# One group's store on GpSimd's queue: three transfers become seven, with other partition counts per DMA engine

## The chip, the cores and the metric

The kernel runs on one core of a Trainium2 chip. Its time is the device time of one execution in microseconds (us); below it is told as the median of several runs. The profile is one further execution, taken by the hardware profiler. Besides the compute engines (TensorE, VectorE, ScalarE, GpSimd and SyncE, in the profile PE, DVE, ACT, POOL and SP) the core has 16 DMA engines. They move all data between the chip's memory and the core's on-chip memory, and every transfer is spread over some or all of them.

## The reference

```python
x: (8, 16, 256, 512) float32      # 128 matrices of 256 x 512
weight: (8, 16, 512, 384) float32 # 128 matrices of 512 x 384
out = np.matmul(x, weight)        # 128 matrices of 256 x 384
```

In all 167.8 MB are read and 50.3 MB are written.

## The kernel before, in words

The 128 matrices are handled in 32 groups of four (`NG = 32`, `G = 4`), numbered n = 0 to 31. For each group SyncE loads 2 MB of x (`load_x`, line 121) and 3 MB of weights (`load_w`, line 138; in two halves for the first four and last two groups). VectorE casts x to bfloat16 (line 194) and, with ScalarE, the weights (lines 207 and 223). TensorE transposes x through PSUM (line 247) and multiplies (line 265, and line 283 for the last group). ScalarE copies the transposed x (line 234) and the products (`copy_out`, line 300) out of PSUM, and the group's 1.5 MB of results are stored (`store`, line 160). The engines run freely beside each other and are held together by semaphores alone.

The order of the transfers is written out by hand in `on_sync`: x of group n + 4, the store of group n, the weights of group n + 4, in a loop; then x and weights of groups 30 and 31; then the stores of groups 27, 28, 29, 30 and 31 (`LAG = 4`). All of these go through SyncE's DMA queue, and each spreads its 128 partitions over the 16 DMA engines, eight partitions to each.

One store is not in that list: that of group 26, the sixth from the end (`SHARED = NG - 2 - LAG = 26`). GpSimd issues it (`store_rest`, lines 164 to 179), when ScalarE has copied the last products of group 26 out and the store of group 25 has landed. It is cut by partitions into three transfers of 5, 120 and 3 partitions. A partition holds 8 rows of 384 numbers, which is 12288 bytes; `max_dma_last_dim` cuts that into two packets of 6144 bytes. Ahead of the first and the third transfer, `reset_dge_cursor` sets back the cursor that says on which DMA engine GpSimd's next transfer begins. All three count up one semaphore, `rest_out`.

The results lie in a ring of four slots (`OS = 4`), so that group 30 writes where group 26 lay. `copy_out` of group 30 therefore waits for `rest_out` to reach 16 for each of the transfers (line 296) before its first copy. GpSimd has nothing to do after `store_rest`.

At the end, SyncE waits for the landing of the stores of groups 28 to 30 (`o_end`, line 329), counts a spare semaphore up some times (lines 330 to 333, `PAD = 12`), and waits for the landing of the last store (`o_fin`).

Of the kernel before, what the change touches and what calls it, by code (L numbers as in the profile page):

```python
# [12 lines left out]
def kernel(  # L13
# [10 lines left out]
    _, _, _, N = weight.shape  # L24
# [18 lines left out]
    R = G * M // P  # L43
    T = R // 2
    SH, SL = 2, 4
    NG = B // G
# [5 lines left out]
    LAG = 4  # L52
# [6 lines left out]

    PAD = 12  # L60

    SHARED = NG - 2 - LAG

    ctx.enter_context(tc.tile_critical(sync_engine=mybir.EngineType.Pool, no_gpsimd_drain=True))  # L64

    def sbuf(name, shape, dtype, n):
        return [
            ctx.enter_context(nc.sbuf_tensor(f"{name}{s}", shape, dtype)) for s in range(n)
        ]
# [6 lines left out]
    def sems(name, n):  # L76
        return [tc.alloc_semaphore(f"{name}{s}") for s in range(n)]
# [9 lines left out]
    out_sb = sbuf("out_sb", [P, OS * R, N], fp32, 1)[0]  # L87
# [16 lines left out]
    rest_out = sems("rest_out", 1)[0]  # L104
# [59 lines left out]
    def store_rest(e):  # L164
        n = SHARED
        e.wait_ge(o_copied, n * T + T + BIAS)
        e.wait_ge(o_out[(n - 1) % 2], 16 + 16 * ((n + 1) // 2))
        dram = o_rows[n * G * M : (n + 1) * G * M].rearrange("(p r) n -> p r n", r=R)
        a = slot(0, NG, n) * R
        p = 0  # L170
        for k, reset in ((5, True), (120, False), (3, True)):
            if reset:
                e.inc_swdge_sem([], [], mode="reset_dge_cursor")
            e.dma_start(  # L174
                out=dram[p : p + k],
                in_=out_sb[p : p + k, a : a + R],
                max_dma_last_dim=R // 2 * N * 4,
            ).then_inc(rest_out, 16)
            p += k

    def is_shared(n):
        return isinstance(n, int) and n == SHARED

    def slot(t, U, s):
        return (t * U + s) % OS
# [106 lines left out]
    def copy_out(e, t, U, s, q):  # L292
        n = t * U + s
        if q == 0:
            if isinstance(n, int) and is_shared(n - OS):
                e.wait_ge(rest_out, 16 * 3)
            elif not isinstance(n, int) or n >= OS:
                e.wait_ge(o_out[s % 2], (t * (U // 2) + s // 2) * 16 + (16 - OS // 2 * 16 + 16))
        e.wait_ge(p_made, n * T + (q + 1 + BIAS))
        e.copy(  # L300
            out=out_sb[:, bass.ds(slot(t, U, s) * R + 2 * q, 2), :],
            in_=po[(s * T + q) % PO][:, :, :N],
        ).then_inc(o_copied, 1)

    def on_gpsimd(e):
        e.memset(identity[:], 0.0).then_inc(id_done, 1)  # L306
        e.wait_ge(id_done, 1)
        make_identity(nc, identity[:], nomemset=True)
        e.drain().then_inc(id_done, 1)
        store_rest(e)  # L310
# [70 lines left out]
    def on_scalar(e):  # L381
# [8 lines left out]
        def step(t, U, s):  # L390
            short = is_short(t * U + s + 1)
            evacuate(e, t, U, s + 1, range(T - 1))
            for q in range(T):
                copy_out(e, t, U, s, q)
                if q == 0:
                    evacuate(e, t, U, s + 1, range(T - 1, T))
                if q == 0 and short:
                    e.sem_inc(w_acast, CA)
                if q > 0 and not short:
                    last = CA if q == T - 1 else q  # L400
                    cast_w(e, t, U, s + 1, range(CV + q - 1, CV + last), q == 1)
# [11 lines left out]
        for q in range(T):  # L413
            copy_out(e, 0, NG, NG - 1, q)
# [36 lines left out]
```

## Time and profile before

| what | value |
|---|---|
| median of 3 runs | 515.9 us (515.87 to 516.13) |
| the profiled execution | 515.93 us, of which the span from first to last instruction is 514.2 us |
| busy share of the span | ScalarE 80%, VectorE 77%, TensorE 61%, GpSimd 1% |
| moved by DMA | 218.18 MB, 424 GB/s over the span |
| SyncE's DMA queue | 98.8% of the time of 16 engines over the span |
| GpSimd's DMA queue | 368 packets, 1.57 MB, 0.7% |
| GpSimd's three issues | 460.5 to 463.6 us |
| issue of the last store (SyncE) | 505.50 us |

The table is read so: the page of the profile gives the busy time of each compute engine, and for DMA the time that each queue's packets took, as a share of what 16 engines could have worked in the span. Times in the text are us from the start of the span.

### The profile page before, as it was taken

How to read it: one execution, taken by the hardware profiler on the slowest of the kernel's cores; microseconds unless marked ns; L12 is line 12 of the kernel's file. 1: busy time of each engine (PE TensorE's matmuls, PEld its weight loads, DVE VectorE, ACT ScalarE, POOL GpSimd, SP SyncE). 2: the span in 40 equal slices, each digit the busy share in tenths (PEclk: the TensorE clock that was granted, in tenths of full speed). 3: DMA queues.
4: the chain of work that ended last, by engine and by line, in shares of the span. 5: the costliest groups of instructions: out<-in, count | busy, mean ns of one | idle time of the engine just before them, and what ended most of it. 6: DMA issues, size and time to landing. Idle time of an engine off the chain costs nothing.

```text
span 514.2 us, 11663 instructions
## 1 busy us (share of the span) xinstructions
PE 312.7 (61%) x4512; PEld 220.0 (43%) x4512; DVE 397.6 (77%) x462; ACT 409.6 (80%) x387; POOL 3.8 (1%) x9
## 2 busy tenths in 40 slices
PE   2276737546575656865666754577547576655872
PEld 2254425434354443543444543445434354442551
DVE  2788757797777887778977779777798777887980
ACT  1365577897987997898989799879897987998662
POOL 0000000000000000000000000000000000010000
PEclk9698878777876887686778687878777886878697
DMA  8999999999999999999999999999999999999997
GB/s 335 430 427 422 441 422 425 432 431 437 428 422 434 432 431 435 423 428 433 437 429 433 422 434 434 431 432 422 433 437 434 429 427 429 431 436 421 422 429 306
DMA packets 15686, 218.18 MB, mean 424 GB/s; under 512 B 1728, under 2 KB 1728, under 8 KB 3008
## 3 DMA queue, kind: packets, MB, share of 16 engines
q1 hardware_dynamic: 15312, 216.54, 98.8%
q0 software_dynamic: 368, 1.57, 0.7%
q8 instruction: 3, 0.05, 0.0%
q14 instruction: 3, 0.02, 0.0%
HBM read 167.77 MB, written 50.33 MB: 424 GB/s over the span
## 4 chain that ended last, share of the span: by engine, by line
DMA 55%; DVE 31%; issue 9%; PE 1%; DVEq 1%; SPq 1%; ACT 0%; POOLq 0%
DMA w_sb<-in_weight_dram 55%; DVE w_bf L207 20%; DVE w_bf L223 5%; DVE x_bf L194 5%; PE po L283 1%; SPq L138 0%; DVEq L358 0%; SPq L121 0%; DVEq L64 0%; DVEq L203 0%; ACT out_sb L300 0%; SPq L133 0%; DVEq L191 0%; DVEq L217 0%; SPq L446 0%
## 5 line engine op out<-in xcount | busy, mean ns | idle before, releaser
L207 DVE CAST w_bf<-w_sb 32x1536 bf16<-32x1536 f32 x286 | 271.9, 951 | 81.7 <-DMA w_sb<-in_weight_dram 70.5
L265 PE MATMUL po<-w_bf,x_t 128*32 128x384 bf16 x3968 | 194.6, 355 | 35.2 <-DVE w_bf L207 23.3
L247 PE MATMUL pt<-identity,x_bf 128*128 128x128 f32 x512 | 113.1, 409 | 155.2 <-DVE x_bf L194 155.2
L207 ACT CAST w_bf<-w_sb 32x1536 bf16<-32x1536 f32 x130 | 190.9, 1468 | 5.1 <-DMA w_sb<-in_weight_dram 2.0
L247 PEld LDWEIGHTS pt<-identity,x_bf 128*128 128x128 f32 x512 | 101.6, 223 | 167.5 <-issue 167.0
L265 PEld LDWEIGHTS po<-w_bf,x_t 128*32 128x32 bf16 x3968 | 115.4, 104 | 112.9 <-issue 50.0
L300 ACT COPY out_sb<-po 128x768 f32 (+1 forms) x128 | 102.4, 800 | 59.3 <-PE po L265 54.1
L234 ACT COPY x_t<-pt 128x1024 bf16<-128x1024 bf16 x128 | 123.5, 1020 | 20.6 <-PE pt L247 20.0
L194 DVE CAST x_bf<-x_sb 128x1024 bf16<-128x1024 f32 x128 | 80.0, 688 | 12.4 <-DMA x_sb<-in_x_dram 11.6
L223 DVE CAST w_bf<-w_sb 64x1536 bf16<-64x1536 f32 x48 | 45.8, 955 | 7.3 <-DMA w_sb<-in_weight_dram 6.0
L234 ACT ACT_TABLE_LOAD x1 | 1.3, 1283 | 10.8 <-PE pt L247 10.8
L174 POOL DMA_DIRECT2D out_dram<-out_sb x3 | 3.1, 1040 | 458.7 <-DMA out_dram<-out_sb 458.7
L283 PE MATMUL po<-w_bf,x_t 128*128 128x384 bf16 x32 | 5.4, 326 | 1.6 <-DVE w_bf L223 1.6
L283 PEld LDWEIGHTS po<-w_bf,x_t 128*128 128x128 bf16 x32 | 3.1, 98 | 3.9 <-issue 1.9
masks.py:199 POOL TENSOR_SCALAR_AFFINE_SELECT identity<-identity 128x128 f32<-128x128 f32 x1 | 0.3, 284 | 0.2 <-POOL identity L306 0.2
L306 POOL MEMSET identity<- 128x128 f32 x1 | 0.2, 205 | 0.5 <-POOLq L64 0.5
L435 POOL MEMSET const-bfloat16-1.0<- 128x1 bf16 x1 | 0.1, 97 | 0.0
L435 POOL MEMSET const-uint8-127<- 128x1 uint8 x1 | 0.1, 97 | 0.0
L435 POOL MEMSET const-float32-0.0<- 128x1 f32 x1 | 0.1, 93 | 0.3 <-issue 0.3
L435 POOL MEMSET const-float32-1.0<- 128x1 f32 x1 | 0.1, 93 | 0.0
## 6 DMA issues: line engine op xcount, KB each, us to landing
w_sb<-in_weight_dram SPq DMA_DIRECT2D x26, 3072.0 KB, 18.1
x_sb<-in_x_dram SPq DMA_DIRECT2D x32, 2048.0 KB, 22.2
out_dram<-out_sb SPq DMA_DIRECT2D x31, 1536.0 KB, 24.9
w_sb<-in_weight_dram SPq DMA_DIRECT2D x12, 1536.0 KB, 16.7
out_dram<-out_sb POOLq DMA_DIRECT2D x1, 1440.0 KB, 17.0
out_dram<-out_sb POOLq DMA_DIRECT2D x1, 60.0 KB, 7.3
out_dram<-out_sb POOLq DMA_DIRECT2D x1, 36.0 KB, 17.9
```

What stands on the lines that cost most here:

```text
L174: e.dma_start(out=dram[p : p + k], in_=out_sb[p : p + k, a : a + R], max_dma_last_dim=R // 2 * N * 4,).then_inc(rest_out, 16)
L194: e.tensor_copy(out=x_bf[s % BS][:, rows].rearrange("p r (s q c) -> p r s q c", s=S, c=KO), in_=x_sb[s % XS][:, rows].rearrange("p r (q s ...
L207: copy(out=w_bf[(s * G + i) % WBS][h * C : (h + 1) * C], in_=w_sb[s % WS][i * C : (i + 1) * C, h * KO : (h + 1) * KO, :],).then_inc(w_vcas ...
L223: e.tensor_copy(out=w_bf[(n * G + d * SH + a) % WBS][h * p : (h + 1) * p], in_=w_sb[n % WS][a * p : (a + 1) * p, r : r + KO, :],).then_inc ...
L234: e.copy(out=x_t[s % TS][:, 2 * q : 2 * q + 2], in_=pt[(s * T + q) % PT][:].bitcast(bf16),).then_inc(t_copied, 1)
L247: ins = e.transpose(pt[(s * T + q) % PT][:, rr, h, :], words[:, 2 * q + rr, h :: KO // 2], identity[:],)
L265: ins = e.matmul(po[(s * T + q) % PO][mine, rr, :N], x_t[s % TS][:, 2 * q + rr, ko // 2, mine, ko % 2], w_bf[(s * G + i) % WBS][:, ko, :], ...
L283: ins = e.matmul(po[(s * T + q) % PO][:, rr, :N], x_t[s % TS][:, 2 * q + rr, ko // 2, :, ko % 2], w_bf[(s * G + q) % WBS][:, ko, :], start ...
L300: e.copy(out=out_sb[:, bass.ds(slot(t, U, s) * R + 2 * q, 2), :], in_=po[(s * T + q) % PO][:, :, :N],).then_inc(o_copied, 1)
L306: e.memset(identity[:], 0.0).then_inc(id_done, 1)
L435: nc = _bacc.Bacc("TRN2", target_bir_lowering=False, num_devices=1)
```

## The change

The 128 partitions of group 26 are cut into seven transfers instead of three. Each line says whether the cursor is set back first, the first partition, the number of partitions, and which of the partition's eight rows are taken. The first five partitions are stored in two halves of four rows each. The wait in `copy_out` counts seven transfers. The few words that come with the change name the engines 1 to 16: engines 13 to 16 get six partitions, 6 to 12 ten, and the first four eight.

```diff
-    SHARED = NG - 2 - LAG
+    SHARED, PARTS = NG - 2 - LAG, 7
...
-        p = 0
-        for k, reset in ((5, True), (120, False), (3, True)):
+        H = R // 2
+        parts = [
+            (True, 0, 5, 0, H),
+            (False, 5, 75, 0, R),
+            (True, 0, 5, H, R),
+            (False, 80, 35, 0, R),
+            (False, 115, 8, 0, R),
+            (True, 123, 4, 0, R),
+            (True, 127, 1, 0, R),
+        ]
+        assert len(parts) == PARTS
+        for reset, p, k, lo, hi in parts:
             if reset:
                 e.inc_swdge_sem([], [], mode="reset_dge_cursor")
             e.dma_start(
-                out=dram[p : p + k],
-                in_=out_sb[p : p + k, a : a + R],
-                max_dma_last_dim=R // 2 * N * 4,
+                out=dram[p : p + k, lo:hi],
+                in_=out_sb[p : p + k, a + lo : a + hi],
+                max_dma_last_dim=(hi - lo) // 2 * N * 4,
             ).then_inc(rest_out, 16)
-            p += k
...
-                e.wait_ge(rest_out, 16 * 3)
+                e.wait_ge(rest_out, 16 * PARTS)
```

## The prediction

> **What bounds the kernel now.** I read the page's DMA rows first.
>
> ```profile
> DMA  8999999999999999999999999999999999999997
> ...
> q1 hardware_dynamic: 15312, 216.54, 98.8%
> q0 software_dynamic: 368, 1.57, 0.7%
> ```
>
> The DMA engines are full in every slice but the first and the last. The bytes are fixed, so time can only be lost where some engines have work left and others have none. That is the end, which the windows show (busy us of PE, PEld, DVE, ACT and POOL, clock, DMA share, GB/s):
>
> ```profile
> 500.00:505.00 5.00, 4.64 (x29) 2.56 (x27) 0.00 (x0) 2.72 (x4) 0.00 (x0) 1.00 1.01 430
> 505.00:510.00 5.00, 0.00 (x0) 0.00 (x0) 0.00 (x0) 0.47 (x1) 0.00 (x0) 0.85 0.96 393
> 510.00:514.20 4.20, 0.00 (x0) 0.00 (x0) 0.00 (x0) 0.00 (x0) 0.00 (x0) 0.50 0.24 96
> ```
>
> No compute engine works after 505.5; 7 us more are DMA. The DMA view of 509.2 to 513.2 (slices of 0.1 us) shows how it ends:
>
> ```profile
> DMA  9999989999984644553331333420200000000000
> ```
>
> All engines work until 510.3, half of them stop within 0.2 us, and the rest go one by one until 512.2. Last come SyncE's end and what GpSimd's store touches, from the timelines and from the waits of SP:
>
> ```profile
> 505.50 0.39 SPq L160 DMA_DIRECT2D out_dram<-out_sb  x1
> ...
> 460.46 3.12 POOL L174 DMA_DIRECT2D out_dram<-out_sb  x3 [458.75 <-DMA out_dram<-out_sb]
> ...
> 493.66 0.80 ACT L300 COPY out_sb<-po 128x768 f32<-128x768 f32 x1 [0.39 <-PE po L265]
> ```
> ```profile
> SPq L330 <- DMA out_dram<-out_sb: 3.0, 1, 3.0
> SPq L333 <- DMA out_dram<-out_sb: 1.3, 1, 1.3
> ```
>
> SP's last two waits are for landings of stores; the very last is for the store issued at 505.50.
>
> **Who is late.** The trace's packet records carry no engine number, but a packet begins where the one before it on its engine ends, so from 460 us on they fall into sixteen chains. Counting GpSimd's packets of 6144 bytes: three chains have 20 (ten partitions), one 18, one 2, eleven 16. This is what the code gives if engines are numbered from 0 at the cursor's reset: 5 partitions on engines 0 to 4; 120 from engine 5 on, eight each on fifteen engines, round to 3; 3 on 0 to 2. So engines 0 to 2 have ten, 3 nine, 4 one, 5 to 15 eight.
>
> Each transfer lands in sixteen steps, one per engine. The last load that landed before GpSimd's packets (weights of group 29, first step at 463.34) had twelve engines within 1.19 us, three 2.44 to 2.55 behind, one 4.11 behind. At the first weights of group 31 (first step 488.04) the three are 2.43 to 2.57 behind: unmoved, so they are among the eleven with eight. The one at 4.11 has dropped into the middle: it is engine 4. Three instruction packets of 16384 bytes (queue q8 of the page; at 15.2, 39.3 and 46.0 us, 1.03 to 1.10 us each, on three chains) make the three late: before the first, two engines trail by 0.7 and 0.8 and none by more; from 48.5 us on exactly three trail by 1.80 to 1.89.
>
> The last store's closing packets then come at 510.36 to 510.52 (eight engines with eight), 510.78, 511.46 and 511.76 (the ten-partition engines), 511.10 and 511.21 (engines 3 and 4), and 512.12, 512.16, 512.24 (the three). The last landing is at 512.69, the span ends 1.48 later.
>
> **The change, part by part.** A packet of 6144 bytes takes its chain 0.231 us (464.923 to 465.154), so a partition costs 0.46 and two 0.92.
>
> *Shares.* By the rule above, a transfer takes the largest number of engines up to 16 that divides its partitions. New: 5 halves on 0 to 4; 75 as five each on 5 to 15 and 0 to 3; 5 halves on 0 to 4; 35 as five each on 5 to 11; 8 as one each on 12 to 15 and 0 to 3; 4 on 0 to 3; 1 on 0. Sum: engine 0 nine, 1 to 3 eight, 4 one, 5 to 11 ten, 12 to 15 six. 9 + 24 + 1 + 70 + 24 = 128.
>
> *Late three.* If they are among 12 to 15, each loses 0.92: 511.20 to 511.32.
>
> *Engines 0 to 4.* Engines 1 and 2 lose 0.92, 0 and 3 lose 0.46: at most 511.76 - 0.46 = 511.30. Engine 4 stays, at most 511.21.
>
> *Engines 5 to 11 gain 0.92.* The eight early engines have slack: at group 30's store their landings are 0, 0.13, 0.20, 0.46, 0.47, 0.66, 0.67 and 0.91 behind the first. The last store, issued at 505.5, holds the foremost: all eight end within 0.17 of each other. Beyond that, lag and end go one to one (lag 0.91 ends at 510.52, 2.5 to 2.63 at 512.12 to 512.24): end = 509.61 + lag. With 0.92 more the last of them ends at 509.61 + 0.91 + 0.92 = 511.44, if it is one of the seven (seven cases in eight), else the next at 511.20. So what is late next is this engine, and the end moves from 512.24 to 511.44: **-0.80 us**, or -0.92 in the eighth case.
>
> *Four more issues.* An issue took 0.94 to 1.15 on POOL; four make 4.2, until about 467.8. The resets cost nothing visible: three issues fill the 3.12 us. POOL has nothing queued behind. ACT's first copy of group 30 (493.66, held by PE) is the only waiter. GpSimd's last packet was at 480.13, on chains with 20 packets, as many as engines 5 to 11 get now; with 4.2 added it is 484.3. That leaves 9 us as cover; were it gone, ACT, the last store and the end would slip one for one.
>
> *Loads behind these packets.* Group 31's halves landed at 490.61 and 494.27, set by the late three; VectorE uses them from 491.18 and 495.09. The loaded seven land at most at 488.88 + 0.92 = 489.80, ahead of that: no new wait. Engine 4 held the weights of group 29 (466.92), with two 0.23 packets ahead; halves bring that forward by up to 0.23, which shifts the last store's issue and not the backlog: nothing.
>
> *Tail.* SP's chain from the landing of group 30's store to its last wait moves along. An instruction packet (8192 bytes, 0.42 us) came at 511.79, on an engine already done; now it comes near 511.0, when about half of the engines still work. Nothing if its engine is early, 0.42 if it is last. I take nothing, since in the row before it delayed no end, and keep 0.42 for the range: -0.38 at worst.
>
> Sum: 515.93 (span 514.2 and 1.73 around it, as good as the median 515.9) - 0.80 = **515.1**; this case's own range is 514.8 to 515.6.
>
> **The rivals.** *A late engine is among the loaded seven (slower).* Its end is 512.24 + 0.92 = 513.16, so 516.85. It decides as soon as one of the three is among engines 5 to 11. For it: nothing in the trace numbers the eleven chains, and scattered at random the three would rarely all hit four places of eleven. Against: the three are alike, each fetched one block of instructions by one queue, and rings of one kind set up one after another lie more likely side by side, at an end of the row, than scattered; that is a guess and the weakest step. Chance 0.2.
>
> *The 35 partitions do not go five each on seven engines.* The old counts, 5, 120 and 3, also fit "partitions over 16, rounded up, per engine": then 35 goes three each on 5 to 15 and two on 0, and 8 on 1 to 8. The late three keep eight, or nine; with eight the end stays at 512.24: 515.9. For it: each of the 11 chains without data in the first transfer still has small filler packets of 4 bytes, as if every transfer were laid out for sixteen. Against: no row. Chance 0.1. The Trainium skill, page "DMA: Bandwidth & Descriptors", section "Why a DMA increments its semaphore by 16 and not by 1", states both: the largest divisor as the rule, with GpSimd's transfers on consecutive engines from a cursor, and as an exception some direct copies from GpSimd with the partitions over 16, rounded up, on each engine. By its rule the sum is 515.1, by its exception 515.9; the trace agrees with the cursor (120 leave out engine 4) and cannot tell the two apart.
>
> *The seven transfers land after 493.66.* ACT would wait and the end slip; it needs 9 us more than the sum above. Chance 0.05.
>
> **How the numbers follow.** Forecast 0.65, rivals 0.2, 0.1 and 0.05. Forecast and unchanged hold 0.75, so the range must take in the slower rival: 514.8 to 516.9. A measurement of this kernel can tell about 0.2% (1.03 us) from no change. The forecast's -0.80 is inside that, and its best case, -0.92, is near the edge; the slower rival's +0.92 likewise. Faster 0.25: a third of the forecast, for ends that drift 0.1 to 0.2 from run to run, and little else. Slower 0.15: nearly half of the slower rival and all of the last. Same 0.6.
>
> **What would show it.** POOL's row with seven issues over 7.3 us; no wait of ACT on DMA at 493; chains with 20 packets of 6144 bytes seven times and 12 four times, and five chains with four packets of 3072 (the halves); the DMA digits full until about 510.8, then gone by 511.5; the last landing at 511.9. Wrong, if the last packet comes at 512.2 or later, or if chains with 6 partitions are not those that trailed before.

## The result, and the profile after

The changed kernel takes 517.19 us (median of 11 runs, 515.5 to 517.36) against 515.9 us before (median of 11, 515.78 to 516.13): a ratio of the means of 1.0021 with a 95% interval of 1.0011 to 1.0030. It is slower by 1.3 us, where 515.1 was forecast.

The median hides two kinds of execution. The profiled one took 515.5, and the ten others 516.67 to 517.36, with nothing between. The profile shows the first kind only. It is read first, with the lines that answer to those of before. The page's DMA rows:

```profile
DMA  8999999999999999999999999999999999999997
...
q1 hardware_dynamic: 15312, 216.54, 98.9%
q0 software_dynamic: 544, 1.57, 0.8%
q8 instruction: 3, 0.05, 0.0%
q14 instruction: 3, 0.02, 0.0%
```

SyncE's queue moves the same packets as before. GpSimd's queue has 544 packets instead of 368 and the same bytes. The windows of the end (busy us of PE, PEld, DVE, ACT and POOL, clock, DMA share, GB/s):

```profile
500.00:505.00 5.00, 4.58 (x29) 2.54 (x26) 0.00 (x0) 2.77 (x4) 0.00 (x0) 1.00 1.01 430
505.00:510.00 5.00, 0.00 (x0) 0.00 (x0) 0.00 (x0) 0.42 (x1) 0.00 (x0) 0.89 0.97 401
510.00:513.70 3.70, 0.00 (x0) 0.00 (x0) 0.00 (x0) 0.00 (x0) 0.00 (x0) 0.50 0.25 99
```

From 505 to 510 the engines move 401 GB/s where it was 393. The DMA view of 509.2 to 513.2, in slices of 0.1 us, shows why:

```profile
DMA  9999999999998885653410000000000000000000
```

Most engines now work until 510.7, and the last packet of data ends at 511.39; before, half stopped by 510.5 and the rest trailed until 512.24. (A digit counts a packet in the slice in which it begins.) That is the balancing that was forecast. The timelines of SP, POOL and ACT:

```profile
505.44 0.39 SPq L160 DMA_DIRECT2D out_dram<-out_sb  x1
...
460.53 5.84 POOL L184 DMA_DIRECT2D out_dram<-out_sb  x7 [458.82 <-DMA out_dram<-out_sb]
...
493.61 0.80 ACT L309 COPY out_sb<-po 128x768 f32<-128x768 f32 x1 [0.39 <-PE po L274]
```

Seven issues fill 5.84 us of POOL; the last store is issued where it was; ACT's first copy of group 30 still waits for PE and not for DMA. SP's last two waits:

```profile
SPq L339 <- DMA out_dram<-out_sb: 2.2, 1, 2.2
SPq L342 <- DMA out_dram<-out_sb: 1.4, 1, 1.4
```

The wait for the stores of groups 28 to 30 is 0.8 us shorter (3.0 before). The last landing is at 511.92, against 512.69. But the span is only 0.44 shorter (513.73, from 514.17). The other 0.33 has gone to a drain, one of GpSimd's last instructions: in the trace's instruction records it starts 0.35 us behind the last landing in both kernels and takes 313 ns before and 640 ns after.

### The profile page after: what moved, and what is told of

The parts are those of the page before. It is cut to its first block, busy times and chain, and to the rows that moved or that the text cites. A ratio compares the mean times of both kernels' runs of the same rounds, so it can differ in the third digit from the quotient of the medians.

```text
span 513.7 us, 11669 instructions
## 1 busy us (share of the span) xinstructions
PE 319.5 (62%) x4512; PEld 222.5 (43%) x4512; DVE 397.6 (77%) x462; ACT 409.4 (80%) x387; POOL 6.5 (1%) x13
## 4 chain that ended last, share of the span: by engine, by line
DMA 55%; DVE 31%; issue 9%; PE 1%; DVEq 1%; SPq 1%; ACT 0%; POOLq 0%
DMA w_sb<-in_weight_dram 55%; DVE w_bf L216 20%; DVE w_bf L232 5%; DVE x_bf L203 5%; PE po L292 1%; SPq L138 0%; DVEq L367 0%; SPq L121 0%; DVEq L64 0%; DVEq L212 0%; ACT out_sb L309 0%; DVEq L200 0%; SPq L133 0%; DVEq L226 0%; SPq L455 0%
## 5 line engine op out<-in xcount | busy, mean ns | idle before, releaser
L274 PE MATMUL po<-w_bf,x_t 128*32 128x384 bf16 x3968 | 200.8, 363 | 33.8 <-DVE w_bf L216 24.1
L274 PEld LDWEIGHTS po<-w_bf,x_t 128*32 128x32 bf16 x3968 | 117.7, 106 | 115.8 <-issue 47.7
L184 POOL DMA_DIRECT2D out_dram<-out_sb x7 | 5.8, 838 | 458.8 <-DMA out_dram<-out_sb 458.8
```

The lines of the kernel that those rows point to most:

```text
L184: e.dma_start(out=dram[p : p + k, lo:hi], in_=out_sb[p : p + k, a + lo : a + hi], max_dma_last_dim=(hi - lo) // 2 * N * 4,).then_inc(rest_ ...
L274: ins = e.matmul(po[(s * T + q) % PO][mine, rr, :N], x_t[s % TS][:, 2 * q + rr, ko // 2, mine, ko % 2], w_bf[(s * G + i) % WBS][:, ko, :], ...
```

## The experiments

Two questions are open: where the second kind of execution comes from, and what lengthens the drain. The theories for the first: (A) in most executions one of the late engines is among engines 5 to 11, which got ten partitions (the prediction's slower rival); (B) the number of transfers does it; (C) the transfer of a single partition does it; (D) a delay comes at random whatever the shares are. Where an expectation uses a letter for a theory, it is one of these. "Shares" below are partitions on engines 0 to 15, counted from the cursor's reset. Every kernel was run beside the kernel before on the same chip; each gives its profiled execution and its other ones.

### The changed kernel once more

No edit.

> The changed kernel once more, to see whether its profiled execution and its timed executions differ again (first time: profiled 515.5 us, ten timed ones 516.67 to 517.36 us). Theory A (the late DMA engines are 12 to 15 in the profiled execution but sit among the loaded engines 5 to 11 in the timed ones): timed about 517.2, and where a profile of a slow execution comes out, its last store lands near 513.6 with the late chains carrying 20 packets. Theory B (the end of the program costs more after seven transfers: GpSimd's last drain took 0.64 us instead of 0.31 in the profile, and could take some 2 us in the timed executions): timed about 517.2, last landing at 511.9 in any profile, and a long drain where the execution is slow.

Profiled 515.64. Of the nine others four took 515.61 to 515.75 and five 516.94 to 517.31; before 516.04; ratio 1.0010 (1.0000 to 1.0019). So both kinds come without a profile too, about 1.5 us apart, and in a mixture that differs: ten of ten others in the first run, five of nine here.

### Eight transfers with the shares of before

```diff
+            (True, 0, 5, 0, H), (False, 5, 75, 0, R), (True, 0, 5, H, R), (False, 80, 33, 0, R),
+            (False, 113, 4, 0, R), (True, 117, 4, 0, R), (True, 121, 4, 0, R), (True, 125, 3, 0, R),
```

> Eight transfers, but each DMA engine has the same partitions as before the change (10, 10, 10, 9, 1 and eleven times 8). Theory A: 515.9 us as before, since only shares matter. Theory B: slower than before by at least as much as the change is, 517.2 to 517.6 us, since there are eight transfers.

Profiled 516.23, all others 516.19 to 516.48; ratio 1.0007 (0.9997 to 1.0016). One kind only. With one transfer more than the change, but shares of 10, 10, 10, 9, 1 and eleven eights, the second kind is gone: the number of transfers does not make it. The DMA view of 509.2 to 513.2 trails as it did before the change:

```profile
DMA  9999999897655536333333336220000000000000
```

The number does cost something. The last landing is at 512.53 (before 512.69), yet the span is 514.4 against 514.2: GpSimd's drain takes 722 ns.

### Five transfers, and six without the single partition

```diff
+five:          (True, 0, 5, 0, R), (False, 5, 75, 0, R), (True, 80, 5, 0, R), (False, 85, 35, 0, R), (False, 120, 8, 0, R),
+six_no_single: (True, 0, 5, 0, H), (False, 5, 75, 0, R), (True, 0, 5, H, R), (False, 80, 35, 0, R),
+               (False, 115, 8, 0, R), (True, 123, 5, 0, R),
```

> The shares of the change (8, 8, 8, 8, then 2, seven times 10, four times 6) from five transfers: no halves and no transfer of one partition; engine 4 has one partition more. Theory A: timed about 517 us like the change. Theory B: between before and the change; if a price per transfer, the tail is half as much longer, about 516 us; profiled end of DMA as in the change, 515.3 to 515.6.

> The change with its last two transfers (4 partitions and 1) put together into one of 5, so that no transfer has a single partition; in the profile of the change the single one had gone out as sixteen packets of 768 bytes. Theory A: about 517 us as the change. Theory B: a little under the change, about 516.9 us, if each transfer costs the same. A third theory, C, that the single partition's transfer is what costs: 515.3 to 515.6 us.

Five: profiled 515.46, others 515.59 and 515.9, then 516.88 to 517.16 five times, and once 517.86; ratio 1.0015 (1.0005 to 1.0025). Six: profiled 515.67, others 515.61 and 515.67, then 516.77 once and 517.02 to 517.18 six times; ratio 1.0013 (1.0004 to 1.0023). Both kinds come with every cut that has these shares, so the single partition is not the cause either. The drains are 477 and 558 ns.

### The heavy shares moved to engines 8 to 14

```diff
+            (True, 0, 5, 0, 4), (False, 5, 75, 0, 8), (True, 0, 5, 4, 8), (False, 80, 3, 0, 8),
+            (False, 83, 35, 0, 8), (False, 118, 5, 0, 8), (True, 123, 5, 0, 8),
```

Shares: 8 four times, 2, then 6 on engines 5 to 7, 10 on 8 to 14, 6 on 15. This puts load on at least two of the three engines that were late in the profiles.

> Seven transfers again, with the ten-partition window moved from engines 5 to 11 onto 8 to 14: shares 8, 8, 8, 8, 2, then 6 for 5 to 7, 10 for 8 to 14, 6 for 15. Theory A (the execution goes one of two ways: the late engines are in 12 to 15, or they are in 5 to 11; where a late engine is loaded the end is two partitions, 0.92 us, after that of before, plus 0.33 of longer drain): the profile, in which 12 to 15 hold the late ones, comes at 517.2 us with late chains that carry 20 packets; if the other place is 5 to 7, the timed executions of the other kind come at 515.5, so values are in two clumps as before but swapped; if it is in 8 to 11, all come at 517.2. Theory D (some engine is delayed by 1.7 us in part of the executions whatever the shares; before the change there is slack that hides it): the profile at 517.2 and no execution at 515.5.

In this first form the halves were cut with `max_dma_last_dim=min(hi - lo, R // 2) * N * 4`, which leaves a half as one run per partition. The cursor then did not move on by five: by the packet chains, engines 3 and 4 got 12 partitions and one engine none. It took 520.41 in the profile (others 520.2 to 520.77; ratio 1.0089, 1.0075 to 1.0102) and tells nothing of engines 8 to 14. It does give a price: engine 4, which at the weights of group 29 lands 3.9 us behind the first, ends last with 12 partitions, and the last landing is at 516.84. With `(hi - lo) // 2 * N * 4`, as in the change:

> The window of 8 to 14 once more, with the halves cut into packets by the change's own rule, so that the cursor moves on by five behind them (in the first try the cursor stayed, and engine 4, the slowest, got twelve partitions): shares 8, 8, 8, 8, 2, then 6 for 5 to 7, 10 for 8 to 14, 6 for 15. Theory A (each execution has its late engines either in 12 to 15 or in 5 to 11; where a late one is loaded the end is 0.92 us after that of before, plus 0.33 of longer drain): the profile at 517.2 us with late chains of 20 packets; executions at 515.5 besides if the other place is 5 to 7, all at 517.2 if it reaches into 8 to 11. Theory D (part of the executions have some engine delayed by 1.7 us, wherever): no execution at 515.5.

Profiled 517.06, all others 517.04 to 517.25; ratio 1.0024 (1.0015 to 1.0033). The faster kind is gone, and the slow case now shows in a trace. The DMA view of 509.2 to 513.2:

```profile
DMA  9999978999988998653231212212112212320100
```

Most engines stop by 510.9, and a few trail until 513.1: the last landing is at 513.48, 0.79 later than before, with a drain of 640 ns as in the changed kernel. Loading a late engine with two partitions more costs nearly what the slower rival said (0.79 us, and not 0.92), and the sum of landing and drain (+0.79 and +0.33 on the 515.93 of the profile before) gives 517.05, where 517.06 was measured. That no execution is at 515.5 does not decide between A and D: both allow for it.

### The heavy shares on engines 5 to 7 alone

```diff
+            (True, 0, 5, 0, 2), (False, 5, 105, 0, 8), (True, 0, 5, 2, 4), (False, 110, 3, 0, 8),
+            (True, 0, 5, 4, 6), (False, 113, 3, 0, 8), (True, 0, 5, 6, 8), (False, 116, 3, 0, 8),
+            (False, 119, 8, 0, 8), (False, 127, 1, 0, 8),
```

> Shares as before the change but for engines 5 to 7, which get ten partitions where 0 to 2 had them: 8, 8, 8, 8, 1, 10, 10, 10, then eight times 8; ten transfers, so the last drain is 0.57 us longer than before. Theory A with the other place at 5 to 7: two clumps, 516.5 (late engines in 12 to 15 and unmoved) and 517.4 (late engines loaded). Theory A with the other place at 8 to 11: one clump at 516.5. Theory D: one clump near 516.5, or values spread up to 517.4 without a gap.

This run had the same flaw in its cut (engine 4 got nine partitions): 519.45 in the profile, others 519.15 to 519.55, ratio 1.0063 (1.0050 to 1.0077). With the flaw mended, the shares are 8 four times, 1, 10 on engines 5 to 7, and 8 on 8 to 15:

> Shares 8, 8, 8, 8, 1, 10, 10, 10, then eight times 8, with the halves' rule mended in the same way; ten transfers, so 0.57 us of longer drain. Theory A with the other place at 5 to 7: two clumps, 516.5 (late engines in 12 to 15) and 517.4 (late engines loaded); with the other place in 8 to 11: 516.5 alone. Theory D: one clump near 516.5 or a spread without a gap. The profile: 516.5, the late three with 16 packets as before.

Profiled 516.84, others 516.6 and 516.73, then 517.25 to 517.53 five times; ratio 1.0024 (1.0013 to 1.0034). Two kinds again, the lower one 0.1 to 0.3 above the 516.5 expected, the upper one about the 517.4. In the profile the three late chains have eight partitions and close the first half of group 31's weights at 489.84 to 490.49, the three loaded ones at 488.50 to 488.78: not one of the late is among 5 to 7 there. In five of the other seven executions one is, by the time. For D, one kind or a spread without a gap was expected; the gap from 516.84 to 517.25 speaks against it, but eight executions do not exclude it.

### Engines 8 to 11, and engines 12 to 15

```diff
+load_12_15: (True, 0, 5, 0, 2), (False, 5, 105, 0, 8), (True, 0, 5, 2, 4), (False, 110, 7, 0, 4), (False, 117, 4, 0, 8),
+            (True, 0, 5, 4, 8), (False, 110, 7, 4, 8), (False, 121, 4, 0, 8), (True, 125, 3, 0, 8),
```

The first kernel has 16 transfers made in the same way, with shares 9, 9, 8, 8, 2, 8 on engines 5 to 7, 10 on 8 to 11, 7 on 12 to 15. The second has 9, 9, 9, 8, 1, 8 on engines 5 to 11, 9 on 12 to 15.

> Shares 9, 9, 8, 8, 2, 8, 8, 8, then 10 for 8 to 11 and 7 for 12 to 15; sixteen transfers, so 1.06 us of longer drain. Executions with the late engines in 12 to 14: 516.5 us. Executions of the other kind: 517.0 if their late engines are in 5 to 7 (with 8, as before the change) and none is in 8 to 11; 517.9 if one is in 8 to 11.

> Shares 9, 9, 9, 8, 1, then 8 for 5 to 11 and 9 for 12 to 15; nine transfers, so 0.49 us of longer drain. Executions with late engines in 12 to 14: 515.95 + 0.46 + 0.49 = 516.9 us. Executions of the other kind: 516.9 too if one of their late engines is still in 12 to 14, so a single clump; 516.4 if none is, so two clumps.

Engines 8 to 11: profiled 516.66, others 517.46, 517.61, 518.02 and 518.20; ratio 1.0035 (1.0022 to 1.0049). The upper two fit a late engine among 8 to 11; 517.5 fits neither case well, a miss. Engines 12 to 15: profiled 516.99, nine others 516.73 to 517.05 and one 516.45; ratio 1.0015 (1.0006 to 1.0024). The last landing is at 513.25 in its profile. So, by the times, a late engine is among 12 to 15 in nearly all executions, though by the runs before most have one in 5 to 7, and some one in 8 to 11.

### The third reset left out, and 5, 105 and 18 partitions

```diff
-        for k, reset in ((5, True), (120, False), (3, True)):
+three_no_reset:  ((5, True), (120, False), (3, False))
+three_5_105_18:  ((5, True), (105, False), (18, True))
```

Two edits of the kernel before. The first gives engines 4 to 6 the last three partitions (shares 9 four times, 2, 9, 9, then 8); the second gives 10 four times, 3, 9 on engines 5 to 8, 7 on the rest.

> The kernel before with one flag changed: the third of the three transfers does not set the cursor back, so its 3 partitions go to engines 4 to 6 instead of 0 to 2: shares 9, 9, 9, 9, 2, 9, 9, then eight with 8 and engine 15 with 8. The drain is as before. If the second kind of execution (a late engine in 5 to 7) is there whatever the number of transfers, and in 5 or 6: two clumps, 515.95 and 516.4 us; if it is engine 7, or comes only with more than three transfers: one clump at 515.95.

> The kernel before with its three transfers cut as 5, 105 and 18 partitions: shares 10 for engines 0 to 3, 3 for engine 4, 9 for 5 to 8 and 7 for 9 to 15; no extra transfer, so no extra drain. Profile, with its late engines in 12 to 14 relieved by one partition: they end at 511.8, engine 4 with two more at about 512.0, so 0.2 us faster than before, 515.8. Executions with a late engine in 5 to 8: 516.4. If the second kind of execution needs more than three transfers, there is one clump at 515.8; if it does not, two clumps, 515.8 and 516.4.

The first: profiled 516.0, others 515.67 to 516.40, before 516.01; ratio 1.0001 (0.9992 to 1.0010). A step of one partition, 0.46 us, is too near the spread of 0.7 us; inconclusive. The second: profiled 516.4, others 515.84 to 516.97, before 515.94; ratio 1.0004 (0.9995 to 1.0013). No gain: in the profile engine 4, which got three partitions, ended last, and the last landing was at 513.15, 0.79 after the landing before it. The 515.8 expected left out that engine 4 stood 4.40 us back at the weights of group 29. That is not all of the 0.79: the engine's last packet ended 0.37 after the next engine's (512.42 and 512.05), and an instruction packet of 0.31 us began just then (512.42).

### More instructions for GpSimd

The late chains in every profile were those with the instruction packets. To see whether such packets make an engine late, the kernel before was given more instructions to fetch:

```diff
+        for _ in range(800):
+            e.sem_inc(more, 1)
         store_rest(e)
```

> The kernel before with its three transfers, but GpSimd first counts a spare semaphore up 800 times, long before its store, so that its instructions need more blocks of 16384 bytes to be fetched. If a fetched block makes its DMA engine late for the rest of the run (1.03 to 1.10 us each in the profiles), some three more fetch packets show up early in the profile, one chain trails by about 3 us more from then on, and all executions come about 1 us or more later than before, about 517, in one clump since the shares of engines 5 to 15 are equal. If fetches don't matter, 515.95.

Profiled 518.5, others 518.36 and 518.43, then 519.52 and 519.62; before 516.08; ratio 1.0056 (1.0042 to 1.0070). The page of this kernel:

```profile
q8 instruction: 3, 0.05, 0.0%
q14 instruction: 9, 0.07, 0.0%
```

Six packets are new. They have 8192 bytes (not the 16384 expected), take 309 to 318 ns each, and come at 9.8, 20.1, 30.6, 40.8, 50.9 and 61.5 us. Over these 50 us, one step of the landings falls back: at the landing before the packets no step is more than 0.70 us behind the first, behind the first packet this one stands at 1.02, then at about 1.7, 2.3, 3.0, 3.7 and 4.2, and at 124 us one engine still trails by 4.2 while no other trails by more than 2.2. So instruction packets do make an engine late, by about 0.65 us for each of 0.31 us, and it does not recover. The timeline of POOL and the DMA view of 509.2 to 513.2 show what that costs:

```profile
461.65 3.10 POOL L175 DMA_DIRECT2D out_dram<-out_sb  x3 [459.92 <-DMA out_dram<-out_sb]
```
```profile
DMA  9999989997989979999999999979972000000000
```

GpSimd's store is issued 1.2 us later than before (460.46), and the engines are full until 512.2 instead of 510.3. The last landing is at 514.93, and the drain, with three transfers, has its 313 ns. And here, with equal shares on engines 5 to 15, there are two kinds, 1.1 us apart: the place of the engine that fetches for GpSimd seems to differ between executions. That is inferred from the times; no trace shows it.

## Why the prediction was wrong, point by point

**Shares: right.** The packet chains of the changed kernel are seven with ten partitions, four with six, four with eight and one with one; the ninth that the prediction gave to engine 0 is the single partition, which went to all sixteen. The 35 go five each on seven engines; the rival of three each falls. With 35 on seven engines the trace now agrees with the divisor rule of the Trainium skill (page "DMA: Bandwidth & Descriptors", section "Why a DMA increments its semaphore by 16 and not by 1"), and not with the exception that it names.

**Late three among 12 to 15: the step that failed.** The sum rests on the "if" of the prediction's *Late three*: that no late engine is among the seven that get ten partitions. It holds in every profile whose shares can tell, and in the profiled execution the late three have six partitions, as forecast; neither sign of being wrong that the prediction named shows there. By the times it fails in most of the executions that were timed without a profile: at least one engine with ten partitions is late in them. Those run to 516.67 to 517.36, which is the slower rival's case: 515.93 + 0.92 + 0.33 = 517.2. The prediction drew the place of the late engines from one trace, called it a guess, and gave the rival 0.2; it was the likelier. The equal shares of the kernel before hide the question: with eight on each of engines 5 to 15 it makes no difference which of them is late, and its runs lie in 0.35 us. What was shown: the two kinds come and go with the shares, and two partitions more on a late engine move the last landing by 0.79 us in a trace (engines 8 to 14; 0.92 was forecast). What was not: no trace of the changed kernel in its slow kind exists, so that a late engine has ten partitions there is inferred from the times.

**Engines 5 to 11: right.** The last packet of data moved from 512.24 to 511.39, by 0.85, where 0.80 was forecast, and the last landing from 512.69 to 511.92, by 0.77.

**Tail: mis-sized.** It was taken as 1.48 us unchanged. The last landing is followed by GpSimd's drain, and that grows with the transfers that GpSimd issued in the program (each column from the runs with so many):

| transfers | 3 | 5 | 6 | 7 | 8 | 9 | 10 | 16 |
|---|---|---|---|---|---|---|---|---|
| drain, ns | 313 | 477 | 558 | 640 | 722 | 803 | 885 | 1375 |

That is 82 ns for each, 0.33 us for the four more. It was a term of the sum at nothing; with the measured landing it gives 515.93 - 0.77 + 0.33 = 515.5 for the profiled kind, which is what it took. The instruction packet, which the prediction took at nothing and kept for the range, seems to have cost 0.1 us. It ran from 511.17 to 511.48, on an engine whose last packet ended at 511.17, and the last landing comes 0.75 after that end. In the five profiles in which such a packet begins just as the engine that is last ends, the last landing comes 0.73 to 0.76 after that end, and in the kernel before 0.45. So the last landing looks to be that engine's; the one before it came at 511.82.

**Issues and waits: right in what they decide.** Seven issues took 5.84 us and not 7.3 (838 ns each, not 0.94 to 1.15). GpSimd's last packet ended at 481.8, far ahead of 493.61. Two details differ: each half of a partition went out as one packet of 6144 bytes and not as two of 3072, and the single partition as 16 packets of 768 bytes, one for each engine.

**What stays open.** Why every profiled execution is of the kind whose late engines are among 12 to 15; and whether in the others the late engines move or more of them are late. A late one shows by the times on engines 5 to 7 in five of seven executions, on 8 to 11 in at least two of four, on 12 to 15 in nine of ten. Three late engines spread over these sets would give that, and so would three among 12 to 15 and further ones elsewhere. By the median, no version beat the kernel before: three transfers with equal shares on engines 5 to 15 end alike wherever the late ones are, and pay the shortest drain.

## What to carry to other kernels

A balance that leans on which engine is late needs that place to be the same in every execution, and one profile cannot show that; look at the single times of the runs, and where they fall into two groups, the profile shows one of them. Cutting one transfer into more is not free even when its issues are hidden: look for what at the end of the program counts them. When a trace cannot number the engines, move the load over one set of them after another and watch which of the time's groups move.

## What the runs showed of the hardware that was not expected

- GpSimd's drain at the program's end takes 82 ns for each transfer it issued, over 313 ns at three (table above), though the transfers had landed 30 us before.
- Instruction packets set their DMA engine back for good in a kernel that keeps all engines full: six of 0.31 us took one engine from at most 0.7 to 4.2 us behind the first, and the kernel took 2.4 us more.
- An instruction packet that begins as an engine ends its last packet puts that engine's landing off: 0.73 to 0.76 us behind the last packet in five profiles (five, six_no_single, three_5_105_18 and the first forms of window_8_14 and load_5_7), 0.45 in the kernel before.
- The cursor depends on how a transfer is cut. Five partitions of two runs each move it by five; five of one run of 6144 bytes did not, and engine 4 got 12 partitions.
- A transfer of one partition (12288 bytes) is spread over all 16 engines in packets of 768 bytes.
